# The gate third of an adaLN read, moved into the latent projections and onto GpSimd

## The chip, the cores and the metric

The kernel runs on one core of one Trainium2 chip. The metric is the device time of one execution in microseconds (us); the time of a kernel is the median over its runs. An execution of the kernel before took 2998.55 us in the median of three.

## What is computed

One layer of a hybrid block for 256 latent tokens and 256 context tokens of width D = 4096, in float32. Cut to what matters here:

```python
mod = silu(c) @ w_ada + b_ada                  # w_ada is 4096 x 12288
shift, scale, gate = split(mod, 3)             # three thirds of 4096
h  = rmsnorm(x) * (1 + scale) + shift          # hc for the context tokens likewise, from c_ctx
xa, xb, ga, gb = split(h @ w_in, 4)            # four of 4096 columns
ya = rglru_branch(xa, xa_c, ...)               # convolution, gates, two scans, 16 heads
yb = pool_branch(xb, ...)                      # centred means, then 4 matrices 1024 x 1024
mixed = concat(ya * silu(ga), yb * silu(gb))
out = rmsnorm(x + gate * (mixed @ w_out))      # w_out is 8192 x 4096
```

`gate` is wanted for the first time when the first block of `mixed @ w_out` is finished. Its third of `w_ada` is 64 MB, read once, for a product of one row: 4096 sums over 4096 weights, each weight times `silu(c)` of its row.

## The kernel before

Weights come in as tiles `raw` of 128 x 1024 float32 (512 KB), through one queue on SyncE (`load_raw`, L91), into a pool of six buffers (`RAWB`). For a matrix product a tile is split in two (`load_w`, L94 to 100): ScalarE rounds it to `hi` (L97, four buffers), and `lo` = `raw` - `hi` is formed by VectorE, or by GpSimd in the xa stage (L99, three buffers). TensorE then multiplies `hi` with 512 columns, of which the second half is the low part of the activations (L566), and `lo` with 256 columns (L567).

The program goes in stages:

1. Start, then the **xa stage** to about 860 us: token statistics, the shift and scale thirds of the adaLN (`ada_units`), and `xa` for both token sets, in nine chunks of the contraction (`xa_units`, L337 to 348). VectorE sums the adaLN products here in PSUM tiles `wide` (L211, L213, L219); GpSimd makes `lo` and adds partial sums (L346). `prep_h` normalizes the activations on VectorE (L300 and, through `split`, L131, tiles `hhi` and `hlo`).
2. **Latent projections**, from about 860 to 2224 us: 384 tiles of `w_in` against the resident `hT` (`pool_units`, `gated_units`), with 32 tiles of the pool matrices and 32 of the recurrent gates. VectorE and ScalarE spread the recurrent branch of 16 heads among them (`lru_pieces`: convolution L459, gates L493, scans L521 to 531), and finish each block of the projections (`fold` L543 to 548, pool sums L597 to 606, gated products L640 and 641).
3. **Output projection**, from 2224 us on: 16 blocks of 16 tiles of `w_out` against `mix`. When a block is done, `out_evac` scales it by `gate` (L696) and sums the squares. At the end the final norm and the stores.

The gate third of the adaLN is 128 tiles in four groups of 1024 columns (`gate_units`). VectorE multiplies and adds each tile into a PSUM tile `wide` (`accumulate`, L206 to 221: the first by L211, then L213, the last in two halves into `fin` by L219). Two products on TensorE bring the 128 partial rows together (L279), ScalarE copies the rows (L185), four products turn them into columns (L192), and VectorE adds the bias into `gate` (L288). Group 0 has its place in the last tenth of the latent projections (`GATE_FROM, GATE_END`, L666), groups 1 to 3 in the output projection, from 8% to 70% of it (`GATE3`, L719 to 725).

`spread` (L49) sets the order by fractions: it lays the entries of one list evenly among those of another. `run` (L102) issues them; it asks for tiles ahead of their use, four for the split weights and two for the adaLN ones (`LOOK`, `LOOK_A`). A scheduler then orders the instructions of each engine by these lists, by data and by free buffers; each engine runs its own queue in order. Pools that matter besides `raw`: 61 `slot` tiles of 128 x 512 in SBUF, four PSUM tiles `mm`, two PSUM tiles `wide`.

Of the kernel before, what the change touches and what calls it, by code (L numbers as in the profile page):

```python
# [13 lines left out]
P = 128  # L14
# [7 lines left out]
GATE3 = (0.08, 0.7)  # L22
GATE_FROM, GATE_END = 0.9, 0.99
# [25 lines left out]
def spread(main, side, lo=0.0, hi=1.0):  # L49
    """Places the entries of side evenly among those of main, from the fraction lo of main to hi."""  # L50
    out, done, n = [], 0, len(main)
    a, b = lo * n, hi * n
    for i, m in enumerate(main):
        out.append(m)
        want = min(len(side), max(0, int((i + 1 - a) / (b - a) * len(side) + 1e-9)))
        while done < want:
            out.append(side[done])
            done += 1
    return out + side[done:]
# [3 lines left out]
def block_kernel(ctx, tc, xc, cvec, vecs, consts, w_ss, w_gate, w_xa, w_lat, w_pool, w_rec, w_out, out):  # L63
# [96 lines left out]
    def rstd_of(ps, r, v, s):  # L160
        """Leaves -2 * rsqrt(ps / D + EPS) in r: one Newton step after the square root."""
        dve.tensor_scalar(out=v, in0=ps, scalar1=1.0 / D, scalar2=EPS, op0=MUL, op1=ADD)
        act.activation(out=s, in_=v, func=AF.Sqrt)
        dve.reciprocal(out=r, in_=s)
        dve.tensor_tensor(out=v, in0=v, in1=r, op=MUL)
        dve.tensor_tensor(out=v, in0=v, in1=r, op=MUL)
        dve.scalar_tensor_tensor(out=r, in0=v, scalar=-3.0, in1=r, op0=ADD, op1=MUL)

# [96 lines left out]
    def gate_units(grp):  # L265
        st = {}

        def unit(k):
            def f(raw):
                if k == 0:  # L270
                    st["accs"] = [wide_tile()]
                    st["fin"] = {}
                accumulate(raw, 0, W, k, st["accs"], 1, 512, st["fin"], k == 0, k == KT - 1)
            return A_(w_gate[grp, k], f)

        def rows():
            r = mm_tile()
            for h in range(2):
                pe.matmul(out=r[0:2, :], lhsT=sel[:, h, 0:2], rhs=st["fin"][h, 0], start=(h == 0), stop=(h == 1))  # L279
            st["rb"] = take_rows(r, 2, 512)  # L280

        def cols():
            o = grp * 8

            def dst(cols):
                g = gate[:, o:o + 8].rearrange("p (h b) -> p b h", h=2)
                bias = vrange("b_ada", 64 + o, 64 + o + 8).rearrange("p (h b) -> p b h", h=2)
                dve.tensor_tensor(out=g, in0=cols, in1=bias, op=ADD)  # L288
            to_cols(st["rb"], 2, 512, dst)
        return [unit(k) for k in range(KT)], S_(rows), S_(cols)  # L290

# [373 lines left out]
    gu, gr, gc = gate_units(0)  # L665
    both = spread(both, gu, GATE_FROM, GATE_END)  # L666
    events += both[:-4] + [gr] + both[-4:-1] + [gc] + both[-1:]

# [50 lines left out]
    side, held = [], []  # L719
    for grp in range(1, 4):  # L720
        gu, gr, gc = gate_units(grp)
        side += gu[:2] + held[:1] + gu[2:4] + held[1:] + gu[4:]
        held = [gr, gc]
    side += held
    events += spread(main, side, GATE3[0], GATE3[1])

# [28 lines left out]
def layout(i):  # L755
# [31 lines left out]
    w_gate = np.ascontiguousarray(w_ada[:, 2 * D:].reshape(KT, P, 4, W).transpose(2, 0, 1, 3))  # L787
# [29 lines left out]
```

## Time and profile before

| | us |
|---|---|
| median of 3 runs (2996.12 to 3000.99) | 2998.55 |
| span of the profiled execution | 2998.8 |
| TensorE busy | 2909.6 (97%) |
| VectorE busy | 2256.7 (75%) |
| ScalarE busy | 1559.9 (52%) |
| GpSimd busy | 530.7 (18%) |
| memory traffic | 679 MB, mean 227 GB/s |

The profiled execution is one run; its span agrees with the median of the runs to 0.3 us, and sums below are made against 2998.8. Engines are called PE (TensorE matmul), PEld (its weight load), DVE (VectorE), ACT (ScalarE), POOL (GpSimd) and SP (SyncE); SPq, DVEq and so on are their queues. L12 is line 12 of the kernel. In a row such as "L99 DVE TENSOR_TENSOR lo<-raw,hi 128x1024 fp32r<-128x1024 f32 x380 | 463.9, 1221 | 189.2 <-PE mm L567 141.2", VectorE made `lo` from `raw` and `hi` 380 times, was busy 463.9 us, 1221 ns a time, and sat idle 189.2 us before these, of which 141.2 ended when the product of L567 was done. Busy time is the time in which at least one instruction was in the engine, so that instructions that follow each other closely overlap a little; waits on a resource inside an instruction count as busy.

### The profile page before, as it was taken

Reading aid. Unit: us, or ns where it says so; the run is one execution under the profiler, and the core shown is the slowest. Engines: PE = TensorE matmul, PEld = TensorE weight load, DVE = VectorE, ACT = ScalarE, POOL = GpSimd, SP = SyncE. Lnnn points to the kernel's source line nnn. Section 1 sums busy time; section 2 is a strip of 40 time slices with the busy share of each in tenths; the row PEclk is TensorE's granted clock in tenths of the full one; section 3 lists DMA queues with packets and bytes.
Section 4 is the critical chain, followed back from the end, with each engine's and each line's share of the span. In section 5 each row is a group of like instructions: output and inputs, shape, how many; then the busy total and the mean of one; then the engine's idle time right before and its main releaser. Section 6 shows DMA issues by size and latency. Waiting matters only on the chain.

```text
span 2998.8 us, 40342 instructions
## 1 busy us (share of the span) xinstructions
PE 2909.6 (97%) x14992; PEld 2405.3 (80%) x14992; DVE 2256.7 (75%) x2661; ACT 1559.9 (52%) x2112; POOL 530.7 (18%) x304
## 2 busy tenths in 40 slices
PE   5999999999999999999999999999999999999997
PEld 2656777778788888888888888888888888878886
DVE  6999999998447788888777777778888766665444
ACT  4442344434436666677666666666464443333442
POOL 1466777777520000000000000000000000000000
PEclk9999999999999999999999999999999999999998
DMA  8777787887365555565665566667978888786665
GB/s 301 279 261 252 262 263 261 272 277 250 126 183 176 176 177 175 179 183 172 186 185 181 185 188 189 196 195 251 326 232 318 318 288 286 264 279 216 193 191 171
DMA packets 201142, 679.47 MB, mean 227 GB/s; under 512 B 22000, under 2 KB 30320, under 8 KB 200944
## 3 DMA queue, kind: packets, MB, share of 16 engines
q1 hardware_dynamic: 200944, 676.89, 68.9%
q8 instruction: 117, 1.92, 0.3%
q14 instruction: 81, 0.66, 0.1%
HBM read 661.60 MB, written 15.20 MB: 226 GB/s over the span
## 4 chain that ended last, share of the span: by engine, by line
PE 84%; DVE 6%; DMA 6%; issue 1%; POOL 1%; ACT 1%; SPq 0%; DVEq 0%; POOLq 0%; ACTq 0%
PE mm L566 38%; PE mm L567 19%; PE mm L337 6%; PE mm L338 6%; PE mm L339 6%; DMA raw<-in_w_gate 4%; DVE wide L213 3%; PE wide L478 2%; PE wide L480 2%; PE wide L479 2%; PE mm L237 2%; DMA raw<-in_w_ss 1%; DMA x<-in_xc 1%; DVE lo L99 1%; DVE hlo L131 1%
## 5 line engine op out<-in xcount | busy, mean ns | idle before, releaser
L97 ACT CAST hi<-raw 128x1024 fp32r<-128x1024 f32 x832 | 871.9, 1049 | 968.6 <-PE mm L566 576.3
L99 DVE TENSOR_TENSOR lo<-raw,hi 128x1024 fp32r<-128x1024 f32 x704 | 856.5, 1221 | 371.5 <-PE mm L567 282.7
L566 PE MATMUL mm<-hT,hi 128*128 128x512 f32 x3072 | 1086.8, 399 | 0.0
L567 PE MATMUL mm<-hT,lo 128*128 128x256 f32 x3072 | 862.7, 281 | 0.0
L213 DVE SCALAR_TENSOR_TENSOR wide<-raw,sc,wide 128x1024 f32<-128x1024 f32 (+1 forms) x556 | 662.4, 1240 | 153.5 <-DMA raw<-in_w_gate 119.6
L566 PE MATMUL mm<-mix,hi 128*128 128x512 f32 x2048 | 724.7, 398 | 0.0
L566 PEld LDWEIGHTS mm<-hT,hi 128*128 128x128 f32 x3072 | 577.2, 188 | 144.5 <-ACT mix L130 0.9
L567 PE MATMUL mm<-mix,lo 128*128 128x256 f32 x2048 | 577.4, 282 | 15.3 <-DVE lo L99 15.1
L567 PEld LDWEIGHTS mm<-hT,lo 128*128 128x128 f32 x3072 | 580.2, 189 | 1.3
L566 PEld LDWEIGHTS mm<-mix,hi 128*128 128x128 f32 x2048 | 386.0, 188 | 95.1 <-ACT hi L97 1.7
L337 PE MATMUL mm<-hhi,hi 128*128 128x512 f32 x1024 | 404.1, 396 | 13.1 <-ACT hhi L130 10.7
L338 PE MATMUL mm<-hlo,hi 128*128 128x512 f32 x1024 | 402.1, 393 | 9.0 <-DVE hlo L131 9.0
L567 PEld LDWEIGHTS mm<-mix,lo 128*128 128x128 f32 x2048 | 388.2, 190 | 20.8 <-DVE lo L99 20.5
L339 PE MATMUL mm<-hhi,lo 128*128 128x512 f32 x1024 | 401.0, 392 | 0.0
L99 POOL TENSOR_TENSOR lo<-raw,hi 128x1024 fp32r<-128x1024 f32 x128 | 310.6, 2427 | 207.5 <-PE mm L339 87.8
L337 PEld LDWEIGHTS mm<-hhi,hi 128*128 128x128 f32 x1024 | 193.4, 189 | 73.0 <-ACT hhi L130 11.8
L346 POOL TENSOR_TENSOR acc<-acc,part 128x512 f32<-128x512 f32 x168 | 221.7, 1331 | 116.8 <-ACT part L345 115.8
L338 PEld LDWEIGHTS mm<-hlo,hi 128*128 128x128 f32 x1024 | 193.6, 189 | 53.3 <-DVE hlo L131 13.4
L339 PEld LDWEIGHTS mm<-hhi,lo 128*128 128x128 f32 x1024 | 193.6, 189 | 42.2 <-issue 1.7
L345 ACT COPY part<-mm 128x512 f32<-128x512 f32 x168 | 97.3, 584 | 155.4 <-PE mm L339 155.0
L348 DVE TENSOR_TENSOR acc<-mm,acc 128x512 f32<-128x512 f32 x88 | 60.1, 685 | 56.6 <-PE mm L339 56.5
L478 PE MATMUL wide<-uhi,hi 128*128 128x512 f32 x256 | 100.5, 393 | 0.0
(134 smaller groups left out, 2203.0 us busy)
## 6 DMA issues: line engine op xcount, KB each, us to landing
raw<-in_w_lat SPq DMA_DIRECT2D x384, 512.0 KB, 3.7
raw<-in_w_ss SPq DMA_DIRECT2D x256, 512.0 KB, 4.6
raw<-in_w_out SPq DMA_DIRECT2D x256, 512.0 KB, 4.6
raw<-in_w_xa SPq DMA_DIRECT2D x128, 512.0 KB, 4.4
raw<-in_w_gate SPq DMA_DIRECT2D x128, 512.0 KB, 4.8
raw<-in_w_rec SPq DMA_DIRECT2D x32, 512.0 KB, 3.6
raw<-in_w_pool SPq DMA_DIRECT2D x32, 512.0 KB, 3.7
x<-in_xc SPq DMA_DIRECT2D x32, 256.0 KB, 6.6
```

The lines of the kernel that those rows point to most:

```text
L97: act.copy(out=hi, in_=raw)
L99: (eng or dve).tensor_tensor(out=lo, in0=raw, in1=hi.bitcast(F32), op=SUB)
L213: dve.scalar_tensor_tensor(out=accs[v][:, :width], in0=seg, scalar=s, in1=accs[v][:, :width], op0=MUL, op1=ADD)
L337: pe.matmul(out=ps, lhsT=wh, rhs=a, start=(k == 0), stop=False)
L338: pe.matmul(out=ps, lhsT=wh, rhs=b, start=False, stop=False)
L339: pe.matmul(out=ps, lhsT=wl, rhs=a, start=False, stop=(k == n - 1))
L345: act.copy(out=part, in_=ps)
L346: nc.gpsimd.tensor_tensor(out=acc[o], in0=acc[o], in1=part, op=ADD)
L348: dve.tensor_tensor(out=acc[o], in0=ps, in1=acc[o], op=ADD)
L478: pe.matmul(out=o, lhsT=wh[:, g, k, m], rhs=st["hi"][k], start=(k == 0), stop=False)
L566: pe.matmul(out=ps, lhsT=hi[:, k, m], rhs=a, start=first, stop=False)
L567: pe.matmul(out=ps[:, 0:T], lhsT=lo[:, k, m], rhs=a[:, 0:T], start=False, stop=last)
```

## The change

The gate third is now 128 tiles of another cut (`layout`): eight groups of 512 columns, sixteen tiles each, and a tile holds two 128-row pieces side by side. A group is summed on GpSimd in a `slot` tile `gacc` in SBUF. For each of the 32 pieces there is a multiplication of 128 x 512 by a column (in place, in the `raw` tile; the first of a group into `gacc`) and, but for the first, an addition to `gacc`. So a tile costs GpSimd four instructions. Four products with a column of ones then give the columns directly (`cols`), and VectorE adds the bias. All eight groups are laid among the latent projections, from 6% to 94% of that list; the output projection has its own 256 tiles alone.

```diff
-GATE3 = (0.08, 0.7)
-GATE_FROM, GATE_END = 0.9, 0.99
+GATE_FROM, GATE_END = 0.06, 0.94
...
     def gate_units(grp):
         st = {}
-
-        def unit(k):
+        half = W // 2
+
+        def unit(i):
             def f(raw):
-                if k == 0:
-                    st["accs"] = [wide_tile()]
-                    st["fin"] = {}
-                accumulate(raw, 0, W, k, st["accs"], 1, 512, st["fin"], k == 0, k == KT - 1)
-            return A_(w_gate[grp, k], f)
-
-        def rows():
-            r = mm_tile()
-            for h in range(2):
-                pe.matmul(out=r[0:2, :], lhsT=sel[:, h, 0:2], rhs=st["fin"][h, 0], start=(h == 0), stop=(h == 1))
-            st["rb"] = take_rows(r, 2, 512)
+                if i == 0:
+                    st["acc"] = slot("gacc")
+                for j in range(2):
+                    k = 2 * i + j
+                    seg, s = raw[:, j * half:(j + 1) * half], sc6[:, k, 2:3]
+                    dst = st["acc"] if k == 0 else seg
+                    nc.gpsimd.tensor_scalar(out=dst, in0=seg, scalar1=s, scalar2=None, op0=MUL)
+                    if k > 0:
+                        nc.gpsimd.tensor_tensor(out=st["acc"], in0=st["acc"], in1=seg, op=ADD)
+            return A_(w_gate[grp, i], f)
 
         def cols():
-            o = grp * 8
-
-            def dst(cols):
...
-            to_cols(st["rb"], 2, 512, dst)
-        return [unit(k) for k in range(KT)], S_(rows), S_(cols)
+            c = mm_tile()
+            for b in range(4):
+                pe.matmul(out=c[:, b:b + 1], lhsT=st["acc"][:, b * P:(b + 1) * P], rhs=ones[:, 0:1],
+                          start=True, stop=True)
+            o = grp * 4
+            dve.tensor_tensor(out=gate[:, o:o + 4], in0=c[:, 0:4], in1=vrange("b_ada", 64 + o, 68 + o), op=ADD)
+        return [unit(i) for i in range(KT // 2)] + [S_(cols)]
...
-    gu, gr, gc = gate_units(0)
-    both = spread(both, gu, GATE_FROM, GATE_END)
-    events += both[:-4] + [gr] + both[-4:-1] + [gc] + both[-1:]
+    gates = [u for grp in range(8) for u in gate_units(grp)]
+    events += spread(both, gates, GATE_FROM, GATE_END)
...
-    side, held = [], []
-    for grp in range(1, 4):
-        gu, gr, gc = gate_units(grp)
-        side += gu[:2] + held[:1] + gu[2:4] + held[1:] + gu[4:]
-        held = [gr, gc]
-    side += held
-    events += spread(main, side, GATE3[0], GATE3[1])
+    events += main
...
-    w_gate = np.ascontiguousarray(w_ada[:, 2 * D:].reshape(KT, P, 4, W).transpose(2, 0, 1, 3))
+    w_gate = np.ascontiguousarray(w_ada[:, 2 * D:].reshape(KT // 2, 2, P, 8, W // 2).transpose(3, 0, 2, 1, 4)).reshape(8, KT // 2, P, W)
```

Some lines shift: what is L99 before is L98 after, L91 is L90, L548 is L546, L566 and L567 are L564 and L565, L696 and L703 are L693 and L700.

GpSimd's queue, end of the program, before: the last things it does are the `lo` tiles of the xa stage.

```order
L99 TENSOR_TENSOR lo<-raw,hi 128x1024 x10
L580 MEMSET pad 128x320
L99 TENSOR_TENSOR lo<-raw,hi 128x1024
L580 MEMSET pad 128x320
L99 TENSOR_TENSOR lo<-raw,hi 128x1024 x3
L812 UNCONDITIONAL_BRANCH
```

The same place after, and on through the latent projections (L276 is the multiplication, L278 the addition):

```order
L98 TENSOR_TENSOR lo<-raw,hi 128x1024 x3
L276 TENSOR_SCALAR gacc<-raw,sc_90 128x512
L278 TENSOR_TENSOR gacc<-gacc,raw 128x512 x3
L276 TENSOR_SCALAR raw<-raw,sc_90 128x512 x2
L278 TENSOR_TENSOR gacc<-gacc,raw 128x512 x2
```

The last two of these rows repeat through the eight groups, two multiplications and two additions a tile. Where a group begins, the multiplications of up to three tiles stand ahead of the first write to the new `gacc`; those of the first group's first two tiles stand in the last rows of the xa stage.

SyncE's queue in the latent projections, before: weights alone, with the spilled heads.

```order
L91 DMA raw<-in_w_lat 128x1024 x7
L91 DMA raw<-in_w_rec 128x1024
L91 DMA raw<-in_w_lat 128x1024 x4
L91 DMA raw<-in_w_pool 128x1024 x8
```

After, from the same place on: a gate tile behind about every third weight tile. The first two are asked for at the end of the xa stage, the third stands behind 34 and the last behind 405 of the 448 weight tiles of this stage.

```order
L90 DMA raw<-in_w_gate 128x1024
L90 DMA raw<-in_w_lat 128x1024 x3
L90 DMA raw<-in_w_gate 128x1024
L90 DMA raw<-in_w_lat 128x1024 x2
L90 DMA raw<-in_w_rec 128x1024
L90 DMA raw<-in_w_gate 128x1024
L90 DMA raw<-in_w_lat 128x1024 x2
```

VectorE's queue in the middle of the output projection, before: a multiply-add of a gate tile after every one or two `lo`.

```order
L213 SCALAR_TENSOR_TENSOR wide<-raw,sc_90,wide 128x1024
L99 TENSOR_TENSOR lo<-raw,hi 128x1024 x2
L213 SCALAR_TENSOR_TENSOR wide<-raw,sc_90,wide 128x1024
L99 TENSOR_TENSOR lo<-raw,hi 128x1024
L213 SCALAR_TENSOR_TENSOR wide<-raw,sc_90,wide 128x1024
```

After, one whole block of it: the `lo` tiles and the finish of a block.

```order
L98 TENSOR_TENSOR lo<-raw,hi 128x1024 x14
L546 TENSOR_TENSOR ov<-mm,fold 128x256
L693 SCALAR_TENSOR_TENSOR xr<-ov,gate,xr 128x256
L98 TENSOR_TENSOR lo<-raw,hi 128x1024
L700 TENSOR_TENSOR ssum<-ssum,ov 128x256
```

The order of the weight products on TensorE is the same in both; the eight sets of four small products (`mm<-ones,gacc 128x1 x4`, L284) lie among those of the latent projections, each behind the last addition of its group.

## Rows read from the trace of the kernel before

**Rows 1.** The page: busy time, and the span in 40 slices of 75 us.
```profile
PE 2909.6 (97%) x14992; PEld 2405.3 (80%) x14992; DVE 2256.7 (75%) x2661; ACT 1559.9 (52%) x2112; POOL 530.7 (18%) x304
...
PE   5999999999999999999999999999999999999997
...
POOL 1466777777520000000000000000000000000000
```

**Rows 2.** The page: shares of the chain of waits by engine.
```profile
PE 84%; DVE 6%; DMA 6%; issue 1%; POOL 1%; ACT 1%; SPq 0%; DVEq 0%; POOLq 0%; ACTq 0%
```

**Rows 3.** Windows by stage: start and end, length, busy time (instructions), granted clock, DMA share, GB/s.
```profile
930.00:1400.00 470.00, 470.00 (x2579) 404.59 (x2578) 385.75 (x567) 318.85 (x418) 0.00 (x0) 1.00 0.58 177
1400.00:2080.00 680.00, 680.00 (x3732) 585.46 (x3732) 501.86 (x639) 463.17 (x599) 0.00 (x0) 1.00 0.62 191
2080.00:2224.00 144.00, 143.98 (x802) 122.84 (x801) 121.20 (x161) 82.59 (x132) 0.00 (x0) 1.00 0.86 293
2224.00:2800.00 576.00, 560.70 (x3136) 479.93 (x3135) 385.38 (x401) 238.51 (x294) 0.00 (x0) 0.99 0.81 274
2800.00:2976.00 176.00, 176.00 (x998) 152.61 (x997) 81.50 (x80) 68.77 (x79) 0.00 (x0) 1.00 0.59 184
```

**Rows 4.** Groups by line in the output projection, 2224 to 2977 us.
```profile
L99 DVE TENSOR_TENSOR lo<-raw,hi 128x1024 fp32r<-128x1024 f32 x254 | 307.3, 1222 | 158.7 <-PE mm L567 130.2 <-issue 21.3 <-ACT hi L97 4.2
...
L213 DVE SCALAR_TENSOR_TENSOR wide<-raw,sc,wide 128x1024 f32<-128x1024 f32 x90 | 115.9, 1287 | 107.2 <-DMA raw<-in_w_gate 106.9
```

**Rows 5.** Windows of the output projection: TensorE's instructions on the tiles mix alone.
```profile
2224.00:2800.00 576.00, 552.71 (x3098) 0.99 0.81 274
2800.00:2976.00 176.00, 176.00 (x998) 1.00 0.59 184
```

**Rows 6.** Groups by line, TensorE, 2200 to 2740 us: small products of four groups.
```profile
L279 PE MATMUL mm<-fin,cst 128*2 128x512 f32 x16 | 7.5, 592 | 0.0
L192 PE MATMUL mm<-cst,rows 2*128 2x2 f32 x32 | 4.2, 249 | 0.0
```

**Rows 7.** Groups by line, GpSimd, whole span.
```profile
L99 POOL TENSOR_TENSOR lo<-raw,hi 128x1024 fp32r<-128x1024 f32 x128 | 310.6, 2427 | 207.5 <-PE mm L339 87.8 <-ACT hi L97 54.0 <-POOL acc L346 51.8
L346 POOL TENSOR_TENSOR acc<-acc,part 128x512 f32<-128x512 f32 x168 | 221.7, 1331 | 116.8 <-ACT part L345 115.8
L580 POOL MEMSET pad<- 128x320 f32 x2 | 0.7, 374 | 0.5 <-DMA xa_sp<-acc 0.5
...
L143 POOL MEMSET ones<- 128x128 f32 x1 | 0.2, 205 | 0.3 <-POOLq L806 0.3
```

**Rows 8.** By line and by tile: xcount, least/median/longest ns, first and last start.
```profile
L91 SPq DMA_DIRECT2D raw<-in_w_lat x384: 327/328/424, 839.8 to 2204.6; - x192
...
L99 POOL TENSOR_TENSOR lo<-raw,hi x128: 2344/2411/2942, 51.1 to 853.7; 128x1024 fp32r<-128x1024 f32 x128
...
L346 POOL TENSOR_TENSOR acc<-acc,part x168: 1264/1297/2194, 129.2 to 780.5; 128x512 f32<-128x512 f32 x168
```

**Rows 9.** Groups by line, VectorE, latent projections, 930 to 2080 us.
```profile
L522 DVE TENSOR_TENSOR i<-i,t 128x512 f32<-128x512 f32 x60 | 41.3, 688 | 1.4
...
L529 DVE TENSOR_TENSOR_SCAN t<-r,i 128x512 f32<-128x512 f32 x30 | 36.6, 1220 | 0.3
...
L526 DVE TENSOR_TENSOR_SCAN ya<-r,t,i 128x256 f32<-128x256 f32 x29 | 21.3, 744 | 0.3
...
L524 DVE TENSOR_TENSOR_SCAN t<-r,i 128x256 f32<-128x256 f32 x29 | 19.9, 686 | 0.2
```

**Rows 10.** Groups by line, VectorE, xa stage, 75 to 790 us.
```profile
L131 DVE TENSOR_TENSOR hlo<-x,hhi 128x512 fp32r<-128x512 f32 x30 | 40.5, 1350 | 6.6 <-ACT hhi L130 6.6
L348 DVE TENSOR_TENSOR acc<-mm,acc 128x512 f32<-128x512 f32 x58 | 39.5, 683 | 16.6 <-PE mm L339 16.5
```

**Rows 11.** Timeline of VectorE, 139.5 to 148 us: start, length, instructions merged.
```profile
139.88 7.95 DVE L300 TENSOR_TENSOR x<-x,rstd 128x512 f32<-128x512 f32 x4
```

**Rows 12.** Timeline of GpSimd, 139 to 148 us.
```profile
138.45 4.36 POOL L346 TENSOR_TENSOR acc<-acc,part 128x512 f32<-128x512 f32 x3 [2.24 <-ACT part L345]
142.76 2.84 POOL L99 TENSOR_TENSOR lo<-raw,hi 128x1024 fp32r<-128x1024 f32 x1
146.00 2.96 POOL L346 TENSOR_TENSOR acc<-acc,part 128x512 f32<-128x512 f32 x2 [0.40 <-ACT part L345]
```

**Rows 13.** Timeline of all engines, 640 to 700 us: VectorE beside GpSimd.
```profile
641.58 8.44 DVE L213 SCALAR_TENSOR_TENSOR wide<-raw,sc,wide 128x1024 f32<-128x1024 f32 x7 [0.39 <-DMA raw<-in_w_ss]
...
644.68 2.41 POOL L99 TENSOR_TENSOR lo<-raw,hi 128x1024 fp32r<-128x1024 f32 x1 [0.80 <-POOL acc L346]
```

**Rows 14.** Windows, VectorE's instructions on the PSUM tiles mm alone: the folds.
```profile
930.00:1400.00 470.00, 21.50 (x53) 1.00 0.58 177
1400.00:2080.00 680.00, 24.19 (x58) 1.00 0.62 191
```

**Rows 15.** The page: DMA issues, median us from issue to landing.
```profile
raw<-in_w_gate SPq DMA_DIRECT2D x128, 512.0 KB, 4.8
```

More of the change, by code (lines that the diff above doesn't have):

```diff
@@ L266, in gate_units @@
         st = {}
-        def unit(k):
+        half = W // 2
+        def unit(i):
             def f(raw):
-                if k == 0:
-                    st["accs"] = [wide_tile()]
-                    st["fin"] = {}
-                accumulate(raw, 0, W, k, st["accs"], 1, 512, st["fin"], k == 0, k == KT - 1)
-            return A_(w_gate[grp, k], f)
-        def rows():
-            r = mm_tile()
-            for h in range(2):
-                pe.matmul(out=r[0:2, :], lhsT=sel[:, h, 0:2], rhs=st["fin"][h, 0], start=(h == 0), stop=(h == 1))
-            st["rb"] = take_rows(r, 2, 512)
-        def cols():
-            o = grp * 8
-            def dst(cols):
-                g = gate[:, o:o + 8].rearrange("p (h b) -> p b h", h=2)
-                bias = vrange("b_ada", 64 + o, 64 + o + 8).rearrange("p (h b) -> p b h", h=2)
-                dve.tensor_tensor(out=g, in0=cols, in1=bias, op=ADD)
-            to_cols(st["rb"], 2, 512, dst)
-        return [unit(k) for k in range(KT)], S_(rows), S_(cols)
+                if i == 0:
[8 more added lines that the diff above has]
+            return A_(w_gate[grp, i], f)
+        def cols():
+            c = mm_tile()
[5 more added lines that the diff above has]
+        return [unit(i) for i in range(KT // 2)] + [S_(cols)]
     hT = [None] * KT
```

## The prediction, made before the result
> **What bounds the kernel now.** I read the page first: TensorE is busy in nearly every slice from the second to the last but one, and the chain of waits lies on it for 84% of the span [rows 1, 2]. So time is won only where TensorE waits, and lost wherever another engine keeps weights from it. The third thing to see on the page is GpSimd: it works in the first twelve slices and does nothing after [rows 1].
>
> The windows by stage tell the two places of the change apart [rows 3]. From 930 to 2080 us, in the latent projections, TensorE has no gap, and VectorE is busy 385.8 of 470 us and then 501.9 of 680 us: 82% and 74%. It isn't the bound, but it has only 84 and 178 us free. From 2224 to 2800 us, in the output projection with its gate tiles, TensorE falls to 560.7 of 576; from 2800 us on, where no gate tile is left, it is full again.
>
> Why TensorE waits there, the groups by line tell [rows 4]: VectorE sat idle 106.9 us until a gate tile landed, with `lo` tiles queued behind it. A landing takes 4.8 us [rows 15], and with six `raw` buffers for both kinds of tile it isn't always asked for early enough.
>
> **What the change takes away.** In the output projection TensorE issues 4096 instructions on `mix`, in 752 us; at the pace of the last 176 us (998 of them) they need 4096 / 998 x 176 = 722 us [rows 5]. So 30 us are to be had, if the pace of the end holds throughout: nothing but weight tiles is left in the queues there. Three of the four groups' small products are in these 30. All four take 7.5 + 4.2 = 11.7 us [rows 6], so group 0, which stands ahead of 2224 us, gives 2.9 more. The eight new sets of four products are like the four of L192 in rows and weight loads, 4.2 / 4 = 1.05 us a set [rows 6]: 8.4 us come back. Their sum: 30 + 2.9 - 8.4 = **24.5 us gained**. VectorE also loses 128 multiply-adds; after 2080 us, where it had group 0, TensorE was full already [rows 3], so that gives nothing.
>
> **What it adds.** The 448 weight loads of the stage go out from 840 to 2205 us [rows 8], 3.05 us apart. By the order 126 of the 128 gate loads stand behind the 34th to the 405th of them, so between some 940 and 2080 us; I take 930 to 2080: one in 9.1 us, 51.6 in the first stretch and 74.7 in the second. Each is two additions and two multiplications of 128 x 512 on GpSimd.
>
> The addition has its row: 1.30 us, with waits of its own left out by the median [rows 8]. The multiplication has none. Below, it is a memset, which reads nothing: 374 ns for 320 columns and 205 for 128 make 0.88 ns a column, 0.54 us for 512 [rows 7]. Above, it is the addition, which reads two inputs: 1.30 us. A subtraction of 1024 columns takes 2411 ns, an addition of 512 takes 1297 [rows 8]: 2.18 ns a column beside a fixed 0.18 us. With one input for two I halve the slope, 512 x 1.09 + 180 = **0.74 us**; that lies between the ends, nearer the memset. A tile then takes 2 x 1.30 + 2 x 0.74 = 4.1 us of GpSimd, under half of the 9.1. GpSimd itself is no bound.
>
> But GpSimd doesn't work beside VectorE for free. An instruction of VectorE on 128 x 512 with both inputs in SBUF takes 688 ns in the latent projections, where GpSimd is idle [rows 9]; `hlo`, of the same size and kind, takes 1350 in the xa stage, where GpSimd works [rows 10]. One that reads PSUM doesn't mind: `acc` from `mm` takes 683 there [rows 10], and seven multiply-adds into `wide` follow each other at 1.21 us each while GpSimd subtracts [rows 13]. The price is seen at 139.88 us, where four multiplications of VectorE in SBUF took 7.95 us [rows 11]. Closely following each other they would take 4 x 0.61 = 2.44 (688 ns less the overlap of 75 that seven multiply-adds show, 1.21 apart at 1.28 each [rows 4, 13]). In those 7.95 us GpSimd got through three additions and a subtraction, taking turns with VectorE, one of its own after one of the other's [rows 12]: 3 x 1.30 + 2.41 = 6.3 us by their usual times. So VectorE lost 5.5 us to 6.3 us of GpSimd: **0.87 of what GpSimd does is added to VectorE's time**, as long as VectorE has such work waiting.
>
> And it does: of VectorE's work in the latent projections only the folds read PSUM, 21.5 and 24.2 us [rows 14]. A tile's price on VectorE is 0.87 x (2 x 1.30 + 2 x 0.74) = 3.55 us; with the multiplication at 0.54 it is 3.20, at 1.30 it is 4.52. GpSimd can use the time of the folds for about 40% of it (9 and 10 us). The demand on VectorE becomes
> - 930 to 1400: 385.8 + 51.6 x 3.55 - 9 = 560 us, against 470: **+90 us**
> - 1400 to 2080: 501.9 + 74.7 x 3.55 - 10 = 757 us, against 680: **+77 us**
>
> VectorE becomes the bound of this stage, and TensorE waits for `lo`. The sum: 2998.8 + 90 + 77 - 24.5 = **3141 us**. With the multiplication at 0.54 us it is +72 and +51, 3097; at 1.30 us +140 and +150, 3264. The ends take VectorE as never idle; waits that can't be filled push up.
>
> One more term hangs on rows I don't have: no scan (L521 to 531) met GpSimd in this trace. Scans take 36.6 + 21.3 + 19.9 = 78 us of the two stretches [rows 9]. If they were as free as the folds, GpSimd could use 40% of them, and 31 us would go: 3110. I count them as contested, since they read two tiles from SBUF like the rest. The Trainium skill (SBUF — State Buffer, "SBUF: two separate sides") puts it as a lock on the port pair that the two engines share, taken for a whole instruction, against any VectorE instruction with two SBUF inputs; by that rule the scans are contested, and the trace's `hlo` and `acc` agree with it (1350 and 683 ns). The skill's GPSIMD Engine Reference, "Engine selection", calls work with one input on GpSimd roughly line-rate; by that the multiplication would be some 0.43 us beside a fixed part (an estimate from its 1.2 GHz), near the low end.
>
> ScalarE does nothing new but loses four copies. SyncE's queue carries the same 128 gate loads, now behind every third weight load; memory moved 177 to 191 GB/s in this stage and 274 to 293 in others [rows 3], so 64 MB more over 1150 us (56 GB/s) fit.
>
> **The rivals.**
> - *The taking of turns stays hidden.* VectorE has 84 / 51.6 = 1.6 us free per gate tile in the first stretch and 178 / 74.7 = 2.4 us in the second [rows 3]. If a tile cost it less than that, TensorE would stay full and only the gain be seen: 2998.8 - 24.5 = 2974 us, **faster**. For it: most of VectorE's instructions might fall where GpSimd rests, since it works 4.1 us of 9.1. Against it: the least price above is 3.20 us, twice and 1.3 times the free time, and a turn taken from a busy VectorE is lost whenever it comes. Chance 0.09, and 0.03 for something between that ends within 0.2% of before (about 6 us, what a measurement can tell from no change).
> - *TensorE waits for the columns.* The four products of a group stand in TensorE's queue behind its last addition, and weight products behind them. GpSimd needs 4.1 us a tile and four waits for a VectorE instruction of 0.8 us in the mean (501.9 / 639 [rows 3]), 7.3 of 9.1 us; it keeps up, but has to wait for a `slot` at each new group. If each wait set it back one tile that it doesn't make up, seven times 9.1 us come on top: 3205 us. Chance 0.06.
> - *The weights lack `raw` buffers.* Where a group begins, up to three gate tiles wait in `raw`, and three of six are left. In the output projection, with a gate tile for 1.66 weight tiles, TensorE lost 30 of 752 us; with one for 3.1 it would lose half the rate, 2% of 1150 us, 23 us on top: 3164. Chance 0.05, and it may hide under the wait for VectorE.
>
> **How the numbers follow.** The forecast, VectorE as the bound by taking turns, has a chance of 0.77; its own range is 3097 to 3264. The others have 0.09, 0.03, 0.06 and 0.05. For 8 in 10 I leave out the hidden case with the 0.03 and the top of the dearest multiplication, and go below 3097 for turns that fall in VectorE's free time or scans that cost nothing: 3050 to 3245. Faster by over 0.2%: 0.09; within: 0.03; slower: 0.88.
>
> **What would show it.** In the windows of the latent projections VectorE should be busy over 95%, and TensorE below 92%, with its waits ended by `lo`. `lo` (1221 ns before) and the other SBUF instructions should have a longer mean, some by 1 us, the folds their old 420 ns. The multiplications should show between 0.54 and 1.30 us when nothing is in their way. The latent projections should end about 165 us later, and the output projection take about 722 us. I am wrong if `lo` keeps its 1.22 us beside a busy GpSimd, if TensorE stays full there, or if TensorE's waits are ended by GpSimd or by loads.

## The result, and the profile after

The changed kernel takes 3462.8 us (median of 4 runs) against 2997.3 (4 runs): a ratio of 1.155, interval 1.153 to 1.157. It is slower by 465 us, over three times the 143 that I forecast, and far outside my range.

The page of the changed kernel: busy time by engine, the slices of TensorE, GpSimd and the granted clock, and groups by line.
```profile
PE 3055.3 (88%) x15008; PEld 2492.6 (72%) x15008; DVE 2328.2 (67%) x2533; ACT 1552.3 (45%) x2108; POOL 1461.7 (42%) x808
...
PE   6999999999987888778787787877779999999997
...
POOL 1566777774055656555555555455550000000000
PEclk9999999999998989989899998988889999999999
...
L96 ACT CAST hi<-raw 128x1024 fp32r<-128x1024 f32 x832 | 871.2, 1048 | 1433.6 <-DMA raw<-in_w_lat 537.6
...
L564 PE MATMUL mm<-hT,hi 128*128 128x512 f32 x3072 | 1179.8, 422 | 91.2 <-ACT hi L96 84.7
L565 PE MATMUL mm<-hT,lo 128*128 128x256 f32 x3072 | 917.6, 299 | 182.4 <-DVE lo L98 181.9
L276 POOL TENSOR_SCALAR raw<-raw,sc 128x512 f32<-128x512 f32 x248 | 509.6, 2065 | 731.7 <-DMA raw<-in_w_gate 455.6
...
L278 POOL TENSOR_TENSOR gacc<-gacc,raw 128x512 f32<-128x512 f32 x248 | 406.5, 1639 | 10.5
```
Windows by stage; the columns are those of [rows 3], the fifth being VectorE. The latent projections now end at 2718 us.
```profile
930.00:1400.00 470.00, 389.57 (x1921) 324.46 (x1921) 347.31 (x419) 233.88 (x310) 258.26 (x143) 0.91 0.49 171
1400.00:2080.00 680.00, 539.88 (x2629) 444.53 (x2629) 447.02 (x483) 319.66 (x420) 385.41 (x204) 0.91 0.46 165
2080.00:2718.00 638.00, 524.88 (x2600) 435.81 (x2599) 392.98 (x434) 302.33 (x413) 276.07 (x154) 0.91 0.50 176
2718.00:3440.00 722.00, 722.00 (x4089) 626.04 (x4088) 359.52 (x379) 306.30 (x371) 0.00 (x0) 1.00 0.64 195
```
All of the loss lies in the latent projections: 2718 in place of 2224. TensorE does 1921 and 2629 instructions where it did 2579 and 3732 [rows 3]. But no engine is its bound: VectorE is busy 74%, 66% and 62%, GpSimd 55%, 57% and 43%, and memory moves less than before. The output projection is full, in some 724 us, as I said (722).

An idle time that belongs to no engine points to a queue. The waits of SyncE's queue between 930 and 2600 us (who it waited for: us in all, times, longest):
```profile
SPq L90 <- POOL gacc L278: 893.1, 125, 10.4
SPq L90 <- DMA raw<-in_w_gate: 389.2, 108, 5.9
SPq L90 <- DVE lo L98: 107.8, 54, 6.1
```
The queue that feeds every weight spends 893 us waiting for GpSimd, 125 times, once per gate tile. The 389 us until a gate tile landed belong to the same waits: the load that takes over its buffer needs the landing first, then GpSimd's work. What this does to TensorE goes through ScalarE. `hi` used to wait for TensorE to free a buffer, as the page of the kernel before has it:
```profile
L97 ACT CAST hi<-raw 128x1024 fp32r<-128x1024 f32 x832 | 871.9, 1049 | 968.6 <-PE mm L566 576.3
```
Now it waits for weights to land (L96 in the page above), VectorE waits for `hi` (201.4 us, below), and TensorE for `lo` and `hi`. The timeline of SyncE's queue and of GpSimd, 1700 to 1730 us, shows how SyncE comes to wait:
```profile
1709.05 0.33 SPq L90 DMA_DIRECT2D raw<-in_w_lat  x1
1709.48 0.37 SPq L90 DMA_DIRECT2D raw<-in_w_gate  x1
1709.96 0.37 SPq L90 DMA_DIRECT2D raw<-in_w_lat  x1
1710.42 0.38 SPq L90 DMA_DIRECT2D raw<-in_w_rec  x1
1722.56 0.33 SPq L90 DMA_DIRECT2D raw<-in_w_lat  x1
1722.98 0.38 SPq L90 DMA_DIRECT2D raw<-in_w_gate  x1
```
```profile
1706.37 2.65 POOL L278 TENSOR_TENSOR gacc<-gacc,raw 128x512 f32<-128x512 f32 x2
1714.11 4.91 POOL L276 TENSOR_SCALAR raw<-raw,sc 128x512 f32<-128x512 f32 x2 [5.09 <-DMA raw<-in_w_gate]
1718.99 3.54 POOL L278 TENSOR_TENSOR gacc<-gacc,raw 128x512 f32<-128x512 f32 x2
```
GpSimd ends a tile at 1709.02; at once a weight load goes out into that tile's buffer and the next gate load behind it. It lands, GpSimd starts at 1714.11 and ends at 1722.53, and only then does SyncE go on, at 1722.56: nothing for 12 us. The reason is the order of the queue, in which the load that reuses a gate tile's buffer stands ahead of the next gate load, here directly (instructions of SyncE; in brackets what they wait for: DMAHW a landing, Pool GpSimd, DVE VectorE):
```
767 L90 DMA raw<-in_w_lat 128x1024 [waits DMAHW6_49,Pool_49]
768 L90 DMA raw<-in_w_gate 128x1024 [waits DMAHW2_49,DVE_49]
```
By the counts that these loads wait for, 109 of 120 gate loads (the first eight left out) can't go out before GpSimd has **finished** the tile before; in the trace 109 do go out after it, 103 of them within 1.5 us. Landing and work, which I took to overlap, follow one another. The gate loads from 930 us to 2560 us (least/median/longest issue, first and last start):
```profile
L90 SPq DMA_DIRECT2D raw<-in_w_gate x124: 327/373/829, 956.7 to 2556.1; - x124
```
(2556.1 - 956.7) / 123 = 13.0 us per tile, where the weights leave room for one in 9.1.

And GpSimd's part is longer than the 4.1 us I gave it: 2 x (2.065 + 1.639) = 7.4 us. By least/median/longest ns:
```profile
L276 POOL TENSOR_SCALAR raw<-raw,sc x248: 1556/1861/3640, 757.1 to 2587.7; 128x512 f32<-128x512 f32 x124
...
L278 POOL TENSOR_TENSOR gacc<-gacc,raw x248: 1252/1530/2392, 927.0 to 2591.6; 128x512 f32<-128x512 f32 x124
```
The multiplication costs 1.56 us with nothing in its way, more than the addition (1.25), not 0.74. The rest, 7.4 - 2 x (1.56 + 1.25) = 1.8 us, is taking turns with VectorE, whose instructions in 930 to 2600 us lengthen in turn (`lo` from 1.22, a scan from 1.22 [rows 4, 9]); the folds from PSUM keep their 0.42:
```profile
L98 DVE TENSOR_TENSOR lo<-raw,hi 128x1024 fp32r<-128x1024 f32 x386 | 522.3, 1357 | 223.5 <-ACT hi L96 201.4 <-issue 9.9 <-PE mm L564 5.9
...
L527 DVE TENSOR_TENSOR_SCAN t<-r,i 128x512 f32<-128x512 f32 x30 | 43.5, 1452 | 0.3
...
L546 DVE TENSOR_TENSOR gv<-mm,fold 128x256 f32<-128x256 f32 x52 | 21.9, 421 | 117.6 <-ACT fold L541 117.6
```

### The profile page after: what moved, and what is told of

It reads as the page before. It is cut to its first block, busy times and chain, and to the rows that moved or that the text cites. A ratio compares the mean times of both kernels' runs of the same rounds, so it can differ in the third digit from the quotient of the medians.

```text
span 3464.3 us, 40956 instructions
## 1 busy us (share of the span) xinstructions
PE 3055.3 (88%) x15008; PEld 2492.6 (72%) x15008; DVE 2328.2 (67%) x2533; ACT 1552.3 (45%) x2108; POOL 1461.7 (42%) x808
## 5 line engine op out<-in xcount | busy, mean ns | idle before, releaser
L96 ACT CAST hi<-raw 128x1024 fp32r<-128x1024 f32 x832 | 871.2, 1048 | 1433.6 <-DMA raw<-in_w_lat 537.6
L98 DVE TENSOR_TENSOR lo<-raw,hi 128x1024 fp32r<-128x1024 f32 x704 | 911.8, 1298 | 622.7 <-PE mm L565 370.2
L564 PE MATMUL mm<-hT,hi 128*128 128x512 f32 x3072 | 1179.8, 422 | 91.2 <-ACT hi L96 84.7
L565 PE MATMUL mm<-hT,lo 128*128 128x256 f32 x3072 | 917.6, 299 | 182.4 <-DVE lo L98 181.9
L276 POOL TENSOR_SCALAR raw<-raw,sc 128x512 f32<-128x512 f32 x248 | 509.6, 2065 | 731.7 <-DMA raw<-in_w_gate 455.6
L564 PEld LDWEIGHTS mm<-hT,hi 128*128 128x128 f32 x3072 | 623.4, 203 | 252.0 <-ACT hi L96 98.5
L565 PEld LDWEIGHTS mm<-hT,lo 128*128 128x128 f32 x3072 | 625.9, 204 | 221.4 <-DVE lo L98 219.7
L564 PE MATMUL mm<-mix,hi 128*128 128x512 f32 x2048 | 723.7, 399 | 0.0
L565 PE MATMUL mm<-mix,lo 128*128 128x256 f32 x2048 | 575.2, 281 | 0.0
L212 DVE SCALAR_TENSOR_TENSOR wide<-raw,sc,wide 128x1024 f32<-128x1024 f32 (+1 forms) x436 | 507.9, 1227 | 30.7 <-DMA raw<-in_w_ss 30.1
L564 PEld LDWEIGHTS mm<-mix,hi 128*128 128x128 f32 x2048 | 384.8, 188 | 96.1
L335 PE MATMUL mm<-hhi,hi 128*128 128x512 f32 x1024 | 403.0, 395 | 13.1 <-ACT hhi L129 10.7
L278 POOL TENSOR_TENSOR gacc<-gacc,raw 128x512 f32<-128x512 f32 x248 | 406.5, 1639 | 10.5
L98 POOL TENSOR_TENSOR lo<-raw,hi 128x1024 fp32r<-128x1024 f32 x128 | 310.9, 2430 | 199.6 <-PE mm L337 84.4
L565 PEld LDWEIGHTS mm<-mix,lo 128*128 128x128 f32 x2048 | 386.9, 189 | 0.0
```

What stands on the lines that cost most here:

```text
L96: act.copy(out=hi, in_=raw)
L98: (eng or dve).tensor_tensor(out=lo, in0=raw, in1=hi.bitcast(F32), op=SUB)
L212: dve.scalar_tensor_tensor(out=accs[v][:, :width], in0=seg, scalar=s, in1=accs[v][:, :width], op0=MUL, op1=ADD)
L276: nc.gpsimd.tensor_scalar(out=dst, in0=seg, scalar1=s, scalar2=None, op0=MUL)
L278: nc.gpsimd.tensor_tensor(out=st["acc"], in0=st["acc"], in1=seg, op=ADD)
L335: pe.matmul(out=ps, lhsT=wh, rhs=a, start=(k == 0), stop=False)
```

## The experiments

The theories, as they came up. TURNS: GpSimd's instructions take VectorE's time (the forecast's mechanism). HOLD: gate tiles keep `raw` buffers too long. LOOP, later ORDER: each gate load waits in SyncE's queue for the tile before, so landing and work are in series. Only `e1_vector` and `e9_late` were timed with an interval; the others were run once, with a profile, beside a run of the kernel before (2995 to 2998 us).

**The sums on VectorE.** In `gate_units`:
```
- nc.gpsimd.tensor_scalar(...) and tensor_tensor(...)
...
+ dve.scalar_tensor_tensor(out=st["acc"], in0=seg, scalar=s, in1=st["acc"], op0=MUL, op1=ADD)
```


> The changed kernel with the sums back on VectorE: one multiply-add of 128x512 for a multiplication and an addition of GpSimd, into the same gacc in SBUF, at the same places in the latent projections. Two theories. HOLD: a gate tile keeps one of six raw buffers while it lands (4.6 us) and while GpSimd works on it (7.4 us as measured), and SyncE's queue stands still behind that buffer, so weights come late. TURNS (the forecast): VectorE loses 0.87 of GpSimd's time. Both expect about the time of the kernel before here, since the tile is held for some 1.5 us of work and GpSimd is idle: VectorE's demand from 930 to 1400 us becomes 385.8 + 51.6 x 1.44 = 460 of 470 us, so 2975 to 3010. Over 3100 would say that it is the place in the program and neither the engine nor the hold.

Measured 2986.9 us, ratio 0.996, interval 0.994 to 0.998. So the places of the loads and the new products are no loss; GpSimd's part is. This version is also 10 us (0.4%) under the kernel before: the latent projections end 27 us later (2251 us for 2224), and the output projection is full and 42 us shorter (710 for 752).
```profile
1400.00:2080.00 680.00, 668.91 (x3660) 571.41 (x3660) 562.99 (x767) 440.99 (x579) 0.00 (x0) 1.00 0.73 239
...
2251.00:2961.00 710.00, 710.00 (x4097) 620.90 (x4096) 359.90 (x382) 307.13 (x371) 0.00 (x0) 1.00 0.65 198
```
With the units at 0.25 to 0.97 of the events (`e9_late`):

> The sums on VectorE in the latent projections (2987 before), with the gate units spread over 0.25 to 0.97 of the events instead of 0.06 to 0.94. If the gate tiles' loads cost by crowding the first part of the stage, 2960 to 2980; if by VectorE's added 185 us wherever they stand, the same 2980 to 2995; denser units (a tile each 7.5 us) may also cost more: up to 3010.

3003.2, ratio 1.0005, interval 0.999 to 1.003, runs from 2985 to 3014: the gain is gone in the median. That the denser packing took it isn't shown. Of the 19 us between the two profiled executions, 9 lie in the latent projections; 13 lie in the output projection, where both have the same instructions. It takes 723 us here, at 398 ns a product (median, `mix` with `hi`), and 710 in `e1_vector`, at 394, with a granted clock of 1.00 in both. No row says why.

**Turns without a hold.**
```
+ seg = hT[k].bitcast(F32)                        # instead of the raw tile
- nc.gpsimd.tensor_scalar(out=dst, in0=seg, ...)
+ nc.gpsimd.tensor_scalar(out=st["acc"], in0=seg, ...)
...                                               # and the addition for every k
```


> The changed kernel, but GpSimd's four instructions for a gate tile read the resident hT and gacc instead of the raw tile; the gate tiles are still loaded and nothing reads them, so the gate is left out of the computation. GpSimd's work and its contention with VectorE stay, the hold of the raw buffer goes. TURNS, with the multiplication at the 1.56 us that the changed kernel shows as its least, expects 0.87 x 5.7 = 5.0 us a tile: +164 and +184 in the two stretches, about 3320. HOLD expects weights on time and 2975 to 3080.

3095.4, between what the two gave (about 3320, and 2975 to 3080). Here the forecast's picture is seen: VectorE is busy 93% in both stretches and TensorE 91 and 92%.
```profile
930.00:1400.00 470.00, 429.85 (x2285) 363.89 (x2284) 439.64 (x491) 279.78 (x373) 367.52 (x184) 0.97 0.63 202
1400.00:2080.00 680.00, 626.64 (x3315) 533.42 (x3314) 631.67 (x590) 398.41 (x522) 606.90 (x313) 0.97 0.66 215
```

**A hold without turns.**
```
- nc.gpsimd.tensor_scalar(...) and tensor_tensor(...)
+ for _ in range(3): nc.gpsimd.memset(raw, 0.0)     # per half: six per tile; eight in e10
```


> The changed kernel, but GpSimd writes zeros over a gate tile six times (128x1024, about 1 us each by 0.88 ns a column) instead of summing it, so the gate is left out of the computation. GpSimd reads nothing from SBUF, but keeps the raw buffer about 5.9 us after the landing, as long as the four instructions do when nothing is in their way (5.7). HOLD expects 3250 to 3460. TURNS expects 2975, if a write alone takes no turn from VectorE.

> As the six memsets per gate tile, but eight: GpSimd writes zeros over the tile eight times and neither multiplies nor adds, so the gate is not computed. The hold of a tile's buffer is then about 8 x 0.957 = 7.7 us, a little over the 7.4 us that the changed kernel's GpSimd needs for a tile, without any lengthening of VectorE's instructions. LOOP (the next gate load stands in SyncE's queue behind a load that waits for GpSimd's release of the tile before, so that landing, GpSimd's work and issue follow one another): 4.4 + 7.7 + 0.4 = 12.5 us per tile, 126 x 12.5 = 1575 us, against 10.9 and 1373 with six memsets, so about 200 us more than 2961: 3100 to 3230. TURNS (GpSimd's reads and writes take VectorE's turns, the hold costs nothing): 2955 to 2990.

2961.3 and 2967.4 us, both under the kernel before: holding a buffer for 6 or 8 us of GpSimd's work costs nothing, and memsets leave `lo` at 1.22. HOLD is dead, and the hold's length, on which I had put LOOP (3100 to 3230 for eight), isn't the point either. Against these floors the turns of `e2_resident` cost some 130 us. The timeline with eight memsets, SyncE's queue and GpSimd:
```profile
1707.96 0.33 SPq L90 DMA_DIRECT2D raw<-in_w_gate  x1
...
1719.07 0.33 SPq L90 DMA_DIRECT2D raw<-in_w_gate  x1
```
```profile
1703.50 8.04 POOL L278 MEMSET raw<- 128x1024 f32 x8 [0.62 <-DMA raw<-in_w_gate]
1712.46 8.04 POOL L278 MEMSET raw<- 128x1024 f32 x8 [0.92 <-issue]
```
The gate load goes out at 1707.96, while GpSimd is at the tile before, and GpSimd starts on the new tile 0.92 us after that one: landing and work overlap. In this program only 12 of 120 gate loads need the tile before finished (109 in the changed kernel): the order written at build time moves with the instructions that GpSimd is given.

**Less work, more buffers, other queues.** Additions only (`e5_addonly`; 111 of 120 in series), two buffers split off for all adaLN tiles (`e4_split`), those loaded from ScalarE's queue (`e6_actq`), seven buffers with temps 14 to 12 (`e7_raw7`; still 98 of 120 in series):
```
e4, e6: rawp bufs=RAWB - 2;  + rawa = tile_pool(name="rawa", bufs=2)   (e6: nc.scalar.dma_start)
e7:     RAWB = 7, temps bufs=12
```


> The changed kernel without GpSimd's multiplications: a tile is added to gacc as it is, two additions instead of four instructions, so the gate is computed without silu(c). LOOP: the load that takes over a gate tile's buffer, and with it the next gate load behind it in SyncE's queue, waits for GpSimd's last addition, so landing (4.6 us) and GpSimd's work (7.4 us a tile in the changed kernel, with turns) add up to 13.2 us a tile against the 9.1 that TensorE needs. With two additions of 1.6 us the loop is 4.6 + 3.3 + some 1.2 = 9.1: 2975 to 3060. TURNS alone, by the forecast's formula without the multiplications (2.26 us a tile), gives +23 and 0, so 2997; the two don't differ much here, but if two additions leave more than 3150 both are wrong.

> The changed kernel with the six raw buffers divided: four for weights and first loads, two for the adaLN tiles, loads still in one queue on SyncE. TURNS expects no change, 3450 to 3480. HOLD by the buffers alone (a weight gets a buffer late since a gate tile sits in it) expects a fall to below 3200; HOLD by the queue (a gate load that waits for its buffer stands in front of the weight loads) expects 3300 to 3480.

> The changed kernel with two of the six raw buffers kept for adaLN tiles and the gate loads issued from ScalarE's queue, so that a gate load that waits for its buffer no longer stands in front of weight loads. GpSimd's work is unchanged. LOOP expects the loss from loads to go and the price of contention to stay, as in the run with resident operands: 3050 to 3150. TURNS expects no change, 3440 to 3480. If ScalarE itself is held up by the waits of its new loads, 3150 to 3400, with ScalarE's casts late.

> The changed kernel with seven raw buffers instead of six (and 12 temps instead of 14, to make room). Between two gate loads there stand three weight loads, so with six buffers the buffer of a gate tile comes up again before the next gate tile is asked for or just then. LOOP expects that one more lets the next gate tile be under way while GpSimd works: 3050 to 3250. TURNS expects no change, 3440 to 3480.

3103.4, 3448.5, 3402.1 and 3440.0: LOOP missed three of the four (it had no number for `e4_split`), and for `e7_raw7` the number is TURNS's. With GpSimd's work halved the loop is 10.2 us, not 9.1, since the landing takes 5.4 in the median; most of the loss goes. A seventh buffer is given to a weight, and the order stays; the fewer temps cost some 37 us with memsets (`e16_temps`, below), so what the buffer alone gives isn't shown. The totals of the two splits mislead: four buffers made the xa stage some 155 us longer, and on ScalarE's queue the blocked load held up `hi`. Counted from the first product on `hT` to the first on `mix`, the latent projections take 1689 us in `e4_split` and 1644 in `e6_actq`, against 1851 in the changed kernel and 1354 before. With buffers apart from those of the weights a part of the loss does go; that `e4_split` ends where TURNS had it is chance.

**Out of place.** The buffer is free after the multiplications:
```
- dst = st["acc"] if k == 0 else seg
+ dst = st["acc"] if k == 0 else temp("gs")
```


> The changed kernel with GpSimd's multiplications written to temp tiles instead of back into raw: the same four instructions and the same result, but the raw tile is free after the two multiplications. LOOP expects the loop to shrink from 4.6 + 7.4 + 1.2 to 4.6 + 4.1 + 1.2 = 9.9 us a tile, 0.8 over TensorE's 9.1: 3050 to 3200. TURNS expects no change, 3440 to 3480.

3129.5: the same arithmetic, the same result, 333 us less, and GpSimd's work is no shorter (2 x (2.23 + 1.66) = 7.8 us a tile). Only 2 of 120 gate loads are in series here. From 930 to 2080 us SyncE waits most for `lo`, and still 356 us for GpSimd's multiplications, of tiles further back:
```profile
SPq L90 <- DVE lo L98: 527.9, 221, 7.5
SPq L90 <- POOL gs L276: 356.5, 75, 8.7
```
```profile
930.00:1400.00 470.00, 421.75 (x2219) 357.10 (x2218) 405.75 (x475) 268.27 (x358) 314.72 (x165) 0.96 0.60 196
1400.00:2080.00 680.00, 625.51 (x3297) 529.25 (x3296) 562.73 (x590) 404.74 (x526) 506.44 (x258) 0.97 0.63 213
```

**Buffers of their own for the gate.** Half tiles in three buffers, temps 11, from GpSimd's queue (`e11_ownq`) and from SyncE's (`e12_ownsp`); whole tiles in two, five `raw` buffers left, temps 12 (`e17_own2`):
```
+ t = ghalf.tile([P, 512], F32, ...); nc.gpsimd.dma_start(out=t, in_=src)   # e12: nc.sync
```


> The changed kernel's arithmetic with the gate tiles halved (128x512), loaded from GpSimd's own queue into three buffers of their own (temps 14 to 11): no load in SyncE's queue waits for GpSimd any more, and the work of GpSimd and its turns with VectorE stay. LOOP: what is left is the turns, 3050 to 3200 (the resident read gave 3095), SyncE's waits for GpSimd gone. TURNS alone as the cause of the 465 us: 3400 to 3480. If the 256 load issues on GpSimd make its work longer than the stage, GpSimd is the last to end and the output projection starts late: 3200 to 3350.

> The same three half-tile buffers, loaded from SyncE's queue: weight loads do not wait for GpSimd, but a gate load that does stands ahead of them in the queue. LOOP: landing and GpSimd's work of two different half tiles overlap now, so a tile costs GpSimd's 7.4 us and not 13.2; the queue is held only when GpSimd is late: 3080 to 3250, dearer than the one with GpSimd's own queue by 0 to 80. TURNS: 3400 to 3480. If the position in the queue alone is what costs, whatever the buffers: 3350 to 3480.

> The changed kernel's own arithmetic, in place, with two buffers of its own for the gate's tiles and five for the rest (temps 14 to 12): a gate load in SyncE's queue needs only the tile before the last finished, so landing and work overlap. ORDER: the turns' loss remains, with one buffer less for weights, 3120 to 3280. TURNS as the whole cause: 3420 to 3500.

3297.7, 3331.0 and 3312.3: each above what ORDER gave, below what TURNS gave. The first falls in the range I had for GpSimd as the last to end, but its last addition ends at 2256 us and the output projection begins at 2560. With GpSimd's queue SyncE never waits for GpSimd, and VectorE is busy 90% (611.5 of 680 us), so turns alone cost more there than in `e2_resident`; ScalarE also issues 62 instructions more with temps 11. With SyncE's queue it still waits 516 us of 930 to 2080 for GpSimd in `e17_own2`, now for the tile before the last. The latent projections take 1674, 1709 and 1679 us in the three, against 1851 in the changed kernel and 1525 in `e8_outplace`. I can't split them further; the fewer temps are part of it.

**The series alone.** Eight memsets, one own buffer, temps 12: all 120 gate loads in series, no turns.
```
+ gown = ctx.enter_context(tc.tile_pool(name="gown", bufs=1))
...                                               # the gate tiles come from it
```


> Eight memsets per gate tile (no multiplication, no addition, so the gate is not computed), and one buffer of its own for the gate's tiles, so that each gate load in SyncE's queue needs GpSimd's work on the tile before it finished; temps 14 to 12. ORDER (the serial loop through SyncE's queue is what costs): landing 4.8 + work 8.3 + issue 0.4 = 13.5 us per tile, 126 x 13.5 = 1700 us in place of 1354 for the latent projections, so 3200 to 3350. If the loop does not reach TensorE without VectorE's turns: 2955 to 3010.

> The same eight memsets and the one buffer, but the gate loads are issued from GpSimd's queue: the loop of 13 us per tile stays, and no load in SyncE's queue stands behind it. The gate is not computed. ORDER: the gate is ready at about 930 + 1700 = 2630, before the end, and TensorE does not see it: 2955 to 3030. If the landing and work in series cost wherever they are issued (the output projection waits for the columns): 3200 to 3350.

> Control: eight memsets in the shared buffers as in the run of 2967, temps 14 to 12. The gate is not computed. If the smaller pool costs nothing, 2960 to 2975; what it adds over 2967 is to be taken off the two runs above.

3182.4, 3285.9, control 3004.2. The totals of the first two don't answer: free of the `raw` buffers, the memsets began with the kernel and stood among GpSimd's weights of the xa stage (GpSimd busy 697 of 75 to 860 us, 526 in the control), and 148 and 282 us were lost there. The latent projections alone take 1412 us with the loads in SyncE's queue, 1380 with the same series in GpSimd's queue, and 1381 in the control. That is as ORDER has it, a series costs only where weights stand behind it, but it is a weak test, since 47 and 62 of the 128 tiles had been loaded before. Tied to the end of that stage by one small multiplication per tile:
```
+ nc.gpsimd.tensor_scalar(out=raw[:, 0:8], in0=raw[:, 0:8], scalar1=hT[KT - 1].bitcast(F32)[:, 0:1], ...)
```


> The eight memsets and the one own buffer again, with one multiplication of 128x8 per tile by a column of the last hT, so that no gate tile's work starts before the xa stage ends (the gate is not computed). The queue has 3.7 weight loads per gate load, 121 gate tiles in the stage. ORDER (the loop paces SyncE's queue): 121 x 13.2 = 1600 us for the latent projections in place of 1381 in the control with the same temps (3004): 3150 to 3260. If the loop costs nothing without the turns: 2990 to 3030.

3149.0, 145 us over the control and 1 us under the foot of what ORDER gave. SyncE's wait, 930 to 2080 us, here and in the control:
```profile
SPq L96 <- POOL graw L287: 911.8, 91, 13.0
```
```profile
SPq L90 <- POOL raw L278: 318.3, 116, 6.7
```
The series alone, with VectorE undisturbed (`lo` at 1.22), holds up the stage: 1503 us for 1381 from the first product on `hT` to the first on `mix`, 118 gate tiles 12.7 us apart. Another 36 us are lost in the output projection, where the last gate tiles now fall; the stage begins 13 us earlier than in the control.

**The same order, wider spaced.**
```
- events += spread(both, gates, 0.06, 0.94)
+ events += spread(both + main, gates, 0.04, 0.86)     # main: the output projection too
```


> The changed kernel with one difference: its gate units are spread over both the latent and the output projections (0.04 to 0.86 of their events), 3.7 to 4 weight loads per gate load in place of 2.9. The order rule, the buffers and GpSimd's work are the same. ORDER: 107 gate tiles in the latent projections x 13.1 = 1400 us, which is about what the weights need anyway; what remains is the turns: 3080 to 3220. TURNS as the whole cause: GpSimd takes as many turns as before, a sixth of them in the output projection, where VectorE has room: 3350 to 3440.

3362.5: the number is TURNS's, not ORDER's. The trace doesn't follow TURNS either: VectorE is busy 75 and 71% of the two stretches, and SyncE waits 509 us for GpSimd; 109 of 120 gate loads are in series, as in the changed kernel. ORDER failed in taking 13.1 us per tile as given. With more weights between two gate loads the landing took 6.2 us in place of 4.6, and the tiles come (2555.7 - 956.3) / 102 = 15.7 us apart:
```profile
L90 SPq DMA_DIRECT2D raw<-in_w_gate x103: 327/382/810, 956.3 to 2555.7; - x103
...
raw<-in_w_gate SPq DMA_DIRECT2D x128, 512.0 KB, 6.2
```
Not 107 but 103 gate tiles fall into the latent projections, and 103 x 15.7 = 1617 us is most of their 1698 (867 to 2565). So by its trace the loop still paces them, with a longer period; by its number this run speaks against ORDER.

## Why the prediction was wrong

- **Place and gain: right.** All of the loss is in the latent projections. The output projection gains 28 us (724 for 752), against the 30 I had for its emptier queues. That it is so close is partly luck: the end of the kernel before, from which I took the pace, and the changed kernel both ran at 176 to 177 ns an instruction of TensorE, while most other versions ran the same 4096 in 710 us, at 173.
- **"The multiplication, 0.74 us": failed.** It is 1.56 alone and 2.07 with turns. Halving the slope for one input had no row behind it, and the true value lay above my upper end, so the range couldn't hold it. The Trainium skill (GPSIMD Engine Reference, "Engine selection") led still lower, by my estimate to 0.43 us beside a fixed part. No run agrees; the measurement, 1.56, decides.
- **"GpSimd itself is no bound, 4.1 of 9.1 us": failed.** It holds only if landing and work overlap. I read the order of the loads against the weights, but not which buffer each load takes and whose release it waits for. This is the step that cost most: undoing it alone, with the dear multiplications left in, gives 333 of the 465 us back (`e8_outplace`).
- **The rival "weights lack `raw` buffers", +23 us, 0.05: right place, wrong price.** I counted buffers; what matters is the queue behind a load whose buffer GpSimd still has. A seventh buffer, which my rival would have wanted, gave 23 us of 465, with fewer temps beside it; the changed kernel's own runs lie 16 us apart.
- **TURNS, the forecast: a real term, not the bound.** VectorE was to be busy over 95% and is busy 62 to 74%: kept from work, it could not be the bound. Where weights keep coming (`e2_resident`) it is 93%. My 167 us for it come near the 130 of `e2_resident` over the memset floors, but by two errors that cancel: GpSimd works 7.4 us a tile, not 4.1, and VectorE lost less than 0.87 of it. In `e2_resident` VectorE was busy 286 us more than with eight memsets (2410.5 and 2124.3), for 1009 us of such work: 0.28. By the least times, which is nearer to how I had reckoned, the work is 256 x (1.56 + 1.25) = 719 us and the share 0.40.
- **Scans contested: right**, 1.45 us for 1.22, and the folds free at 0.42. The lock in the Trainium skill (SBUF — State Buffer, "SBUF: two separate sides") has it so for VectorE's instructions with two inputs in SBUF, and the trace agrees.
- **"TensorE's waits ended by `lo`": came true, and would have misled.** 181.9 us of them ended so. But `lo` waits for `hi` there, and `hi` for weights to land: the loop ends at the same engine as the turns. The sign that told them apart was how busy VectorE is.

How the 465 us come about, as an estimate from the rows. The loop is 13.0 us per tile and 9.06 with eight memsets ((2091.9 - 960.0) / 125), where it isn't one: 3.9 us x 125 = 493. Of the 3.9, turns lengthen GpSimd by 1.8, the true multiplication and addition add 5.6 - 4.1 = 1.5, and 0.6 would have been lost even with my 4.1. The output projection gives 28 back. Shown by runs are the ends: hold alone 0, series alone 145 (with 3.7 weights to a gate tile, where the changed kernel has 2.9), turns alone some 130, both together 465 and the 30 or so of floor. They don't add: turns lengthen a loop that has no slack. TensorE's own rate falls too. Its granted clock is 0.91 in the stage, part of it at the lower level (1.2 GHz) after gaps that end with `lo` and `hi`; it was 1.00 (2.4 GHz) before, without gaps [rows 3]. A product on `hT` and `hi` takes 422 ns in the mean, its median being the old 398 and its longest 796; with eight memsets, at 1.00, the mean is 398. In all TensorE is busy 146 us longer than before. How much the slower clock adds beyond the waits was not tried alone, and why the own-buffer versions stay near 3300 is open.

## What to carry to other kernels

Work that moves to an idle engine brings its buffers' release with it: look in the order of the queue for the load that waits for that release, and at what stands behind it. If the next load of the same kind does, landing and work are in series, and the budget is their sum, not the larger. Free a shared buffer at the first instruction that can (here out of place added no instruction and gave 333 us back), and price an operation without a row between ends that include "dearer than the dearest row".

## What the runs showed of the hardware

- On GpSimd a multiplication of 128 x 512 by a column takes 1.56 us at least, an addition of two tiles 1.25, a memset of twice the columns 0.955 in the median (`e10_memset8`).
- Memsets on GpSimd don't disturb VectorE (`lo` 1.22 beside 1024 of them, `e10_memset8`); multiplications and additions do, scans of VectorE included (1.45 us for 1.22, in the changed kernel).
- A 512 KB load lands later the more of them went out just ahead of it. In the changed kernel, 930 to 2080 us, the median landing is 3.7 us with none issued in the 2.5 us before, 4.5 with one, 5.5 with two and 6.5 with three. So the gate tile's median is 3.7 where it goes first (`e18_serial2`), 4.6 in the changed kernel and 6.2 in `e20_spread`, where at 1721 us it goes behind three weights.
